# A hybrid attention layer with product-key experts: later gathers for one block, selection inside the dense experts, and weight buffers in another place

## The chip, the cores and the metric

One NeuronCore of a Trainium2 chip runs the whole layer. The time is device microseconds of one execution; what counts is the median of several. The engines are TensorE (PE; its weight loads are listed as PEld), VectorE (DVE), ScalarE (ACT), GpSimd (POOL) and SyncE (SP, which issues most transfers).

## What is computed

The layer has 1024 tokens of width 1024. Two attentions (differential attention with 8 heads of two maps, and chunked attention with 8 heads) are gated, projected and added to x, which gives h. Then each token is sent through 128 single-neuron experts out of 16384, and a last RMSNorm follows:

```python
def peer(xn, wq, keys, u, v):          # per block of 128 tokens
    q = (xb @ wq).reshape(PEER_BLOCK, PEER_HEADS, 2, PEER_DKEY // 2)
    v1, i1 = lax.top_k(s1, PEER_TOPK)  # scores against two key tables, 16 best of 128 each
    v2, i2 = lax.top_k(s2, PEER_TOPK)
    sc, ci = lax.top_k(cand, PEER_TOPK)            # 16 best sums of pairs
    e = i1[...] * PEER_NKEYS + i2[...]             # 8 heads x 16 experts
    g = jax.nn.softmax(sc, axis=-1)
    hid = jnp.einsum('thkd,td->thk', u[e], xb)     # first layer
    a = gelu(hid) * g
    return jnp.einsum('thk,thkd->td', a, v[e])     # second layer
h = h + peer(rmsnorm(h, norm2_w), ...)
y = rmsnorm(h, final_norm_w)
```

u and v are 16384 x 1024 float32 tables (64 MB each).

## The kernel before, in words

The tokens are eight blocks of 128. The experts are computed in two ways. **Blocks 0, 1, 6 and 7** (SBLK) are sparse: `experts(b)`, L789, gathers for each of the 128 expert slots the 128 rows of u that the tokens of the block chose (one indirect transfer of 512 KB, issued by GpSimd, L803), multiplies it with the tokens and sums along the row into `hid` (DVE, L809), and does the same with v (gather L803, accumulation into `acc` L815). Between the layers stand the gelu (L811) and the product with the gates (L812), behind them `final` (L781), the last norm and the store (L787). So a block has 256 gathers. The gathered rows go through five buffers (GBUFS, tag "ge" of the pool "gath"); `xs2`, `acc`, `hid`, `a` and `junk` have one buffer each. **Blocks 2 to 5** (DBLK) are dense: `dense_experts`, L681, goes through all 16384 experts in 128 chunks of 128. For a chunk SP loads a tile of u (transposed, L194 in `wtile`) and of v (L735); ScalarE and DVE split each into a high and a low part (`split`, L126: a copy to fp32r on ScalarE, L128, and the rest on DVE, L129); PE multiplies u's parts with the tokens' parts (24 matmuls, L136), ScalarE takes the gelu (L748), DVE multiplies with the gate matrix of the chunk (L749), both are split again, and the second layer (L710 and L717, 24 matmuls a chunk on average) adds up in PSUM. v is split in two halves of 512 columns, u in one piece.

The gate matrices are made ahead of this: `choose` (L565) selects the experts of a block on DVE in nine steps (it is a generator that yields after each), and `gates` (L643) turns the selection of a dense block into a matrix with 32 steps of four tokens, each with a copy L671 on ScalarE, and stores it to memory. For a sparse block `choose` ends with the index list `ei` (L639).

The order of the program is written by hand: generators are advanced by `weave` (L52), one step of the main one and so many of the others. After the attentions come `mop(2)` with the gates of blocks 2 and 3, `mop(3)` with the selection of 4 and 5 and their gates (L894, L895; `mop` and the `merge` that it calls make h, its norm and the query scores of two blocks), then the selection of blocks 6 and 7 (L897), the dense experts, and last the sparse blocks one after the other (L899). Below this a scheduler puts each engine's instructions in an order of its own: what stands later in the program may go ahead where an engine would be idle. So the gathers of block 0, last in the program, start some 340 us into the span, and blocks 6 and 7 run beside the dense experts. Each engine then works its list off in order. A tile takes one of the buffers of its tag, and waits for one to come free.

Pools are laid out one after the other: "wp" holds the raw, high and low parts of weights; "yza" and "tkp" hold what the selection needs; "dk" (L686) holds the dense stage's tiles and opens when the pools of the front (`fstack`, L896) are closed.

Of the kernel before, what the change touches and what calls it, by code (L numbers as in the profile page):

```python
# [7 lines left out]
F32 = mybir.dt.float32  # L8
F32R = mybir.dt.float32r
BF16 = mybir.dt.bfloat16  # L10
# [5 lines left out]
P = 128  # L16
# [56 lines left out]
def layer_kernel(ctx, tc, x, w1, w_in, b_gate, lq1, lk1, lq2, lk2, subln, rel,  # L73
# [3 lines left out]
    con = ctx.enter_context(tc.tile_pool(name="con", bufs=1))  # L77
    gp = ctx.enter_context(tc.tile_pool(name="gath", bufs=GBUFS))
    sms = ctx.enter_context(tc.tile_pool(name="sms", bufs=2))
    wp = ctx.enter_context(tc.tile_pool(name="wp", bufs=2))  # L80
    yza = ctx.enter_context(tc.tile_pool(name="yza", bufs=1))
    tkp = ctx.enter_context(tc.tile_pool(name="tkp", bufs=1))
    drp = ctx.enter_context(tc.tile_pool(name="dr", bufs=1, space=bass.MemoryType.DRAM))

    def load(pool, shape, src, name):
# [40 lines left out]
    def split(raw, hi, lo):  # L126

        nc.scalar.copy(hi, raw)  # L128
        nc.vector.tensor_sub(lo, raw, hi.bitcast(F32))  # L129
# [548 lines left out]
        for f in pend:  # L678
            f()

    def dense_experts():  # L681


        T = DT
        with ExitStack() as st:
            dk = st.enter_context(tc.tile_pool(name="dk", bufs=2))  # L686
            smd = st.enter_context(tc.tile_pool(name="smd", bufs=2))
            xh = dk.tile([P, KC, T], F32R, name="x2h", bufs=1)
            xl = dk.tile([P, KC, T], F32R, name="x2l", bufs=1)
            with tc.tile_pool(name="dps0", bufs=2, space=PSUM) as pt:  # L690
                for i, b in enumerate(DBLK):
                    xs = wp.tile([P, KC, P], F32, name="xd", tag="wr", bufs=WBUFS).rearrange("p a b -> p (a b)")
                    nc.sync.dma_start(xs, xn2d[b])
                    for g in range(2):
                        o = pt.tile([P, 512], F32, name="trd", tag="trd")
                        for j in range(4):
                            nc.tensor.transpose(o[:, j * P:(j + 1) * P], xs[:, (4 * g + j) * P:(4 * g + j + 1) * P], ident)
                        dst = (slice(None), slice(4 * g, 4 * g + 4), slice(i * P, (i + 1) * P))
                        split(cols4(o, 4), xh[dst], xl[dst])
            pd = st.enter_context(tc.tile_pool(name="dps", bufs=1, space=PSUM))  # L700
            acc = [[pd.tile([P, 512], F32, name=f"acc{i}{hf}") for hf in range(2)] for i in range(3)]
            rest = dk.tile([P, D], F32, name="rest", bufs=1)
            nc.sync.dma_start(rest, hd[DBLK[3]])

            def second(j, a, b):
                for x, y in ((0, 0), (0, 1), (1, 0)):
                    kw = dict(start=(j == 0 and x == y), stop=(j == NCH - 1 and x == 1))
                    for i in range(3):
                        for hf in range(2):
                            nc.tensor.matmul(acc[i][hf], a[x][:, i * P:(i + 1) * P], b[y][:, hf * 512:hf * 512 + 512], **kw)  # L710

            def fourth(hf, chunks):
                o = pd.tile([P, 512], F32, name="acc3", tag="acc3")
                cs = slice(hf * 512, hf * 512 + 512)
                todo = [(a[x], b[y]) for _, a, b in chunks for x, y in ((0, 0), (0, 1), (1, 0))]
                for n, (aa, bb) in enumerate(todo):
                    nc.tensor.matmul(o, aa[:, 3 * P:4 * P], bb[:, cs], start=(n == 0), stop=(n == len(todo) - 1))  # L717
                nc.vector.tensor_add(rest[:, cs], rest[:, cs], o)

            def sums(chunks):  # L720

                two = len(chunks) == 2
                if two:
                    fourth(0, chunks)
                second(*chunks[-1])
                if two:
                    fourth(1, chunks)
                    chunks.clear()

            chunks = []  # L730
            new = None
            for j in range(NCH):
                uw = wtile(ut[j])
                vr = dk.tile([P, D], F32, name="vr", tag="vr", bufs=RBUFS)
                nc.sync.dma_start(vr, v[j * P:(j + 1) * P, :])  # L735
                vh = dk.tile([P, D], F32R, name="vh", tag="vh", bufs=VBUFS)
                vl = dk.tile([P, D], F32R, name="vl", tag="vl", bufs=VBUFS)
                for hf in range(2):
                    cs = slice(hf * 512, hf * 512 + 512)
                    split(vr[:, cs], vh[:, cs], vl[:, cs])  # L740
                if j % JG == 0:
                    gj = dk.tile([P, T // TB, JG, TB], F32, name="gj", tag="gj")
                    for i in range(T // TB):
                        nc.sync.dma_start(gj[:, i], gdr[i][:, j:j + JG, :])
                ph = pd.tile([P, 512], F32, name="ph", tag="ph")
                mm3(ph, uw, (xh, xl), KC)
                ge = dk.tile([P, T], F32, name="ge", tag="ge")
                nc.scalar.activation(ge, ph, AF.Gelu)  # L748
                nc.vector.tensor_mul(ge.rearrange("p (n t) -> p n t", t=TB), ge.rearrange("p (n t) -> p n t", t=TB),  # L749
                                     gj[:, :, j % JG, :])  # L750
                ah = dk.tile([P, T], F32R, name="ah", tag="ah", bufs=ABUFS)
                al = dk.tile([P, T], F32R, name="al", tag="al", bufs=ABUFS)
                split(ge, ah, al)
                if new:
                    chunks.append(new)
                    sums(chunks)
                new = (j, (ah, al), (vh, vl))
            def last(tag, src):
                t = wp.tile([P, KC, P], F32, name="last", tag=tag).rearrange("p a b -> p (a b)")
                nc.sync.dma_start(t, src)  # L760
                return t

            hxs = [last("wh", hd[b]) for b in DBLK[:2]]
            wfb = last("wl", wf.to_broadcast([P, D]))
            chunks.append(new)
            sums(chunks)
            for i, b in enumerate(DBLK):
                hx = rest
                if i < 3:
                    if i < 2:  # L770
                        hx = hxs[i]
                    else:
                        hx = dk.tile([P, D], F32, name="hx", tag="vr", bufs=RBUFS)
                        nc.sync.dma_start(hx, hd[b])
                    for hf in range(2):
                        dst = hx[:, hf * 512:(hf + 1) * 512]
                        nc.vector.tensor_add(dst, dst, acc[i][hf])
                sq = wp.tile([P, KC, P], F32, name="sq", tag="wr", bufs=WBUFS).rearrange("p a b -> p (a b)")
                final(hx, sq, smd, b * P, wfb)
# [9 lines left out]
    def experts(b):  # L789

        ei, g = idx_of[b]
        K = P
        xs = gp.tile([P, D], F32, name="xs2", tag="xs2", bufs=1)
        nc.sync.dma_start(xs, xn2d[b])
        acc = gp.tile([P, D], F32, name="acc", tag="acc", bufs=1)
        nc.sync.dma_start(acc, hd[b])
        g = g.rearrange("p a b -> p (a b)")
        hid = gp.tile([P, P], F32, name="hid", tag="hid", bufs=1)[:, :K]
        junk = gp.tile([P, D], BF16, name="junk", tag="junk", bufs=1)

        def gather(src, k):
            t = gp.tile([P, D], F32, name="ge", tag="ge")
            nc.gpsimd.indirect_dma_start(out=t, out_offset=None, in_=src,  # L803
                                         in_offset=bass.IndirectOffsetOnAxis(ap=ei[:, k:k + 1], axis=0))
            return t

        for k in range(K):
            t = gather(u, k)
            nc.vector.scalar_tensor_tensor(junk, t, 1.0, xs, op0=OP.mult, op1=OP.mult, accum_out=hid[:, k:k + 1])  # L809
        a = gp.tile([P, P], F32, name="a", tag="a", bufs=1)[:, :K]  # L810
        nc.scalar.activation(a, hid, AF.Gelu)  # L811
        nc.vector.tensor_mul(a, a, g)  # L812
        for k in range(K):
            t = gather(v, k)
            nc.vector.scalar_tensor_tensor(acc, t, a[:, k:k + 1], acc, op0=OP.mult, op1=OP.add)  # L815
        wfb = gp.tile([P, D], F32, name="wfb", tag="ge")
        nc.sync.dma_start(wfb, wf.to_broadcast([P, D]))
        final(acc, junk, sms, b * P, wfb)

    dn = [None, None]  # L820
# [73 lines left out]
            weave(mop(2, mp, yzb), 26, (gates(gk, d1), 32 * len(d1)))  # L894
            weave(mop(3, mp, yza), 26, (chain(sel([4, 5], yzb), gates(gk, d2)), 18 + 32 * len(d2)))  # L895
    fstack.close()  # L896
    run(sel([6, 7], yza))  # L897
    dense_experts()
    for b in SBLK:  # L899
        experts(b)  # L900


# [49 lines left out]
```

## Time and profile before

| | us |
|---|---|
| median of 3 runs | 3390.54 |
| lowest and highest | 3386.21, 3400.17 |
| the profiled execution, its own time | 3385.27 |
| its span, first to last instruction | 3383.5 |
| mean granted clock of TensorE (share of full speed) | 0.955 |

The page of the profile gives the busy time of each engine and the chain of work that ended last, followed back from the last instruction. Busy time can also be read by stretch of the span, together with the granted clock of PE, the share of the 16 DMA engines and the GB/s that they moved. A timeline lists one engine's instructions by start, with the idle time before each and what released it. Names are the program's: out<-in.

### The profile page before, as it was taken

What the parts mean: (1) busy time and instruction counts of PE and PEld (TensorE: products, weight loads), DVE (VectorE), ACT (ScalarE), POOL (GpSimd) and SP (SyncE); (2) the same over time, 40 slices, a digit from 0 to 9 for tenths busy, and PEclk for the clock granted to TensorE, in tenths of its full rate; (3) what the DMA queues carried; (4) which work ended last, traced back from release to release, by engine and by line L of the source; (5) the groups of instructions that cost most, each with busy time, mean ns of one, the idle gap of its engine ahead of it and who ended that gap; (6) DMA issues with size and microseconds to landing.
All of it is one profiled execution on the core that took longest, in us unless ns stands there. A gap on an engine that the chain in (4) does not pass through costs nothing.

```text
span 3383.5 us, 48294 instructions
## 1 busy us (share of the span) xinstructions
PE 3101.4 (92%) x16032; PEld 2548.4 (75%) x16032; DVE 2696.5 (80%) x5848; ACT 1445.1 (43%) x3029; POOL 1249.5 (37%) x1028
## 2 busy tenths in 40 slices
PE   7997689999979886987787699999999999999998
PEld 7986578888857664676676578888888888888886
DVE  4436797777769999888885999888888888898843
ACT  5634433434324544567749833333323323322323
POOL 0000455555544532344100035555555555555400
PEclk9998899999989897998898899999999999999999
DMA  7675999999999975898744579999999999999841
GB/s 240 217 243 192 369 323 352 334 355 333 332 340 356 323 269 176 281 325 332 269 152 151 210 265 356 344 336 335 340 335 353 329 335 338 337 343 341 314 128 69
DMA packets 406122, 987.13 MB, mean 292 GB/s; under 512 B 43184, under 2 KB 188400, under 8 KB 403696
## 3 DMA queue, kind: packets, MB, share of 16 engines
q0 software_dynamic: 147456, 536.94, 44.8%
q1 hardware_dynamic: 258416, 447.11, 38.0%
q8 instruction: 126, 2.06, 0.2%
q14 instruction: 124, 1.02, 0.1%
HBM read 905.72 MB, written 78.15 MB: 291 GB/s over the span
## 4 chain that ended last, share of the span: by engine, by line
PE 75%; DVE 12%; DMA 5%; ACT 4%; issue 3%; POOL 1%; SPq 0%; DVEq 0%; POOLq 0%; ACTq 0%
PE ph L136 21%; PE mm L136 17%; PE acc L710 15%; PE mm L490 7%; PE acc L717 5%; PE sc L347 3%; PE pv L372 3%; PE tr L203 2%; DVE junk L809 1%; DMA ge<-in_u_dram,ei 1%; PE gg L669 1%; DVE acc L815 1%; DVE qs L561 1%; DVE iu L563 1%; DVE iu L560 1%
## 5 line engine op out<-in xcount | busy, mean ns | idle before, releaser
L803 POOL DMA_INDIRECT ge<-in_u_dram,ei x512 | 616.7, 1205 | 1258.1 <-DVE junk L809 380.3
L803 POOL DMA_INDIRECT ge<-in_v_dram,ei x512 | 632.6, 1236 | 686.9 <-DVE acc L815 469.3
L815 DVE SCALAR_TENSOR_TENSOR acc<-ge,a,acc 128x1024 f32<-128x1024 f32 x512 | 655.1, 1279 | 21.6 <-DMA ge<-in_v_dram,ei 15.9
L809 DVE SCALAR_TENSOR_TENSOR junk<-ge,xs 128x1024 bf16<-128x1024 f32 x512 | 624.1, 1219 | 50.9 <-DMA ge<-in_u_dram,ei 44.6
L129 DVE TENSOR_TENSOR wl<-wr,wh 128x1024 fp32r<-128x1024 f32 x232 | 283.4, 1222 | 215.8 <-ACT wh L128 110.7
L128 ACT CAST wh<-wr 128x1024 fp32r<-128x1024 f32 x232 | 243.4, 1049 | 404.8 <-PE ph L136 276.5
L136 PE MATMUL ph<-x2h,wh 128*128 128x512 f32 x1024 | 406.2, 397 | 8.8 <-DVE x2l L129 6.6
L136 PE MATMUL ph<-x2l,wh 128*128 128x512 f32 x1024 | 407.7, 398 | 0.0
L136 PE MATMUL mm<-xh,wh 128*128 128x256 f32 (+1 forms) x1248 | 372.1, 325 | 0.7 <-ACT st L286 0.6
L136 PE MATMUL mm<-xl,wh 128*128 128x256 f32 (+1 forms) x1248 | 367.0, 321 | 1.3 <-DVE xl L232 1.2
L136 PE MATMUL ph<-x2h,wl 128*128 128x512 f32 x1024 | 259.4, 395 | 0.0
L136 PEld LDWEIGHTS mm<-xh,wh 128*128 128x128 f32 x1248 | 237.0, 190 | 24.8 <-ACT st L286 3.1
L128 ACT CAST vh<-vr 128x512 fp32r<-128x512 f32 x256 | 140.0, 618 | 269.3 <-PE acc L717 244.5
L136 PEld LDWEIGHTS mm<-xl,wh 128*128 128x128 f32 x1248 | 236.6, 190 | 21.4 <-DVE xl L232 2.0
L136 PEld LDWEIGHTS ph<-x2h,wh 128*128 128x128 f32 x1024 | 193.4, 189 | 55.5 <-DVE x2l L129 7.0
L136 PE MATMUL mm<-xh,wl 128*128 128x256 f32 (+1 forms) x1248 | 234.5, 324 | 0.0
L136 PEld LDWEIGHTS ph<-x2l,wh 128*128 128x128 f32 x1024 | 193.6, 189 | 47.7
L136 PEld LDWEIGHTS ph<-x2h,wl 128*128 128x128 f32 x1024 | 192.0, 188 | 46.9
L347 PE MATMUL sc<-kt,qt 64*128 64x256 f32 (+3 forms) x608 | 200.7, 529 | 14.5 <-DVE mn L353 9.0
L128 ACT CAST ah<-ge 128x512 fp32r<-128x512 f32 x128 | 79.7, 622 | 294.9 <-DVE ge L749 294.9
L710 PE MATMUL acc<-vh,ah 128*128 128x512 f32 x768 | 198.8, 389 | 0.0
L136 PEld LDWEIGHTS mm<-xh,wl 128*128 128x128 f32 x1248 | 184.8, 190 | 16.8
(203 smaller groups left out, 5733.1 us busy)
## 6 DMA issues: line engine op xcount, KB each, us to landing
vr<-in_v_dram SPq DMA_DIRECT2D x128, 512.0 KB, 6.5
wr<-in_ut_dram SPq DMA_DIRECT2D x128, 512.0 KB, 5.8
wr<-in_w_in_dram SPq DMA_DIRECT2D x104, 512.0 KB, 5.3
gdr<-gst SPq DMA_DIRECT2D x16, 2048.0 KB, 8.7
gj<-gdr SPq DMA_DIRECT2D x512, 64.0 KB, 6.0
wr<-in_w_bd_dram SPq DMA_DIRECT2D x40, 512.0 KB, 4.2
wr<-in_w_out_dram SPq DMA_DIRECT2D x40, 512.0 KB, 7.4
wr<-in_wq_dram SPq DMA_DIRECT2D x40, 512.0 KB, 5.1
```

What stands on the lines that cost most here:

```text
L128: nc.scalar.copy(hi, raw)
L129: nc.vector.tensor_sub(lo, raw, hi.bitcast(F32))
L136: nc.tensor.matmul(o, w[a][:, k, :], xx[b][:, k, :], start=(i == 0), stop=(i == last))
L203: nc.tensor.transpose(o[:, i * P:(i + 1) * P], s, ident)
L347: nc.tensor.matmul(o[:, :k1 - k0], q, k[:, k0:k1], start=True, stop=True)
L372: nc.tensor.matmul(o[:, :P], aT[:, j - c, :], vt[:, v0 + j, :], start=(j == 0), stop=(j == n - 1))
L490: nc.tensor.matmul(o, w[:, k, :], xx[:, k, :], start=(k == 0), stop=(k == K - 1))
L710: nc.tensor.matmul(acc[i][hf], a[x][:, i * P:(i + 1) * P], b[y][:, hf * 512:hf * 512 + 512], **kw)
L717: nc.tensor.matmul(o, aa[:, 3 * P:4 * P], bb[:, cs], start=(n == 0), stop=(n == len(todo) - 1))
L803: nc.gpsimd.indirect_dma_start(out=t, out_offset=None, in_=src, in_offset=bass.IndirectOffsetOnAxis(ap=ei[:, k:k + 1], axis=0))
L809: nc.vector.scalar_tensor_tensor(junk, t, 1.0, xs, op0=OP.mult, op1=OP.mult, accum_out=hid[:, k:k + 1])
L815: nc.vector.scalar_tensor_tensor(acc, t, a[:, k:k + 1], acc, op0=OP.mult, op1=OP.add)
```

## The change

The pool "wp" is opened after "yza" and "tkp". In the dense experts v is split in one piece. The selection of blocks 6 and 7 is no longer run ahead of the dense experts but handed to them, three steps after each chunk's instructions. `experts` becomes a generator with a stop after the first layer and another in the middle of the second; it loads `acc` after the first stop and takes `junk` once more for the last norm. Block 0 runs as before; of block 1 the first layer and 64 gathers of the second follow, then block 6's first layer, the other 64 of block 1, and the rest of blocks 6 and 7.

```diff
@@ -77,9 +77,9 @@
     con = ctx.enter_context(tc.tile_pool(name="con", bufs=1))
     gp = ctx.enter_context(tc.tile_pool(name="gath", bufs=GBUFS))
     sms = ctx.enter_context(tc.tile_pool(name="sms", bufs=2))
-    wp = ctx.enter_context(tc.tile_pool(name="wp", bufs=2))
     yza = ctx.enter_context(tc.tile_pool(name="yza", bufs=1))
     tkp = ctx.enter_context(tc.tile_pool(name="tkp", bufs=1))
+    wp = ctx.enter_context(tc.tile_pool(name="wp", bufs=2))
     drp = ctx.enter_context(tc.tile_pool(name="dr", bufs=1, space=bass.MemoryType.DRAM))
 
     def load(pool, shape, src, name):
@@ -678,7 +678,7 @@
         for f in pend:
             f()
 
-    def dense_experts():
+    def dense_experts(side, per):
 
 
         T = DT
@@ -735,9 +735,7 @@
                 nc.sync.dma_start(vr, v[j * P:(j + 1) * P, :])
                 vh = dk.tile([P, D], F32R, name="vh", tag="vh", bufs=VBUFS)
                 vl = dk.tile([P, D], F32R, name="vl", tag="vl", bufs=VBUFS)
-                for hf in range(2):
-                    cs = slice(hf * 512, hf * 512 + 512)
-                    split(vr[:, cs], vh[:, cs], vl[:, cs])
+                split(vr, vh, vl)
                 if j % JG == 0:
                     gj = dk.tile([P, T // TB, JG, TB], F32, name="gj", tag="gj")
                     for i in range(T // TB):
@@ -755,6 +753,8 @@
                     chunks.append(new)
                     sums(chunks)
                 new = (j, (ah, al), (vh, vl))
+                for _ in range(per):
+                    next(side, None)
             def last(tag, src):
                 t = wp.tile([P, KC, P], F32, name="last", tag=tag).rearrange("p a b -> p (a b)")
                 nc.sync.dma_start(t, src)
@@ -792,8 +792,6 @@
         K = P
         xs = gp.tile([P, D], F32, name="xs2", tag="xs2", bufs=1)
         nc.sync.dma_start(xs, xn2d[b])
-        acc = gp.tile([P, D], F32, name="acc", tag="acc", bufs=1)
-        nc.sync.dma_start(acc, hd[b])
         g = g.rearrange("p a b -> p (a b)")
         hid = gp.tile([P, P], F32, name="hid", tag="hid", bufs=1)[:, :K]
         junk = gp.tile([P, D], BF16, name="junk", tag="junk", bufs=1)
@@ -807,14 +805,20 @@
         for k in range(K):
             t = gather(u, k)
             nc.vector.scalar_tensor_tensor(junk, t, 1.0, xs, op0=OP.mult, op1=OP.mult, accum_out=hid[:, k:k + 1])
+        yield
+        acc = gp.tile([P, D], F32, name="acc", tag="acc", bufs=1)
+        nc.sync.dma_start(acc, hd[b])
         a = gp.tile([P, P], F32, name="a", tag="a", bufs=1)[:, :K]
         nc.scalar.activation(a, hid, AF.Gelu)
         nc.vector.tensor_mul(a, a, g)
         for k in range(K):
+            if k == K // 2:
+                yield
             t = gather(v, k)
             nc.vector.scalar_tensor_tensor(acc, t, a[:, k:k + 1], acc, op0=OP.mult, op1=OP.add)
         wfb = gp.tile([P, D], F32, name="wfb", tag="ge")
         nc.sync.dma_start(wfb, wf.to_broadcast([P, D]))
+        junk = gp.tile([P, D], BF16, name="junk", tag="junk", bufs=1)
         final(acc, junk, sms, b * P, wfb)
 
     dn = [None, None]
@@ -894,10 +898,15 @@
             weave(mop(2, mp, yzb), 26, (gates(gk, d1), 32 * len(d1)))
             weave(mop(3, mp, yza), 26, (chain(sel([4, 5], yzb), gates(gk, d2)), 18 + 32 * len(d2)))
     fstack.close()
-    run(sel([6, 7], yza))
-    dense_experts()
-    for b in SBLK:
-        experts(b)
+    dense_experts(sel([6, 7], yza), 3)
+
+    e0, e1, e6, e7 = (experts(b) for b in SBLK)
+    run(e0)
+    next(e1)
+    next(e1)
+    next(e6)
+    for e in (e1, e6, e7):
+        run(e)
 
 
 # ---- launch: one core; inputs and outputs as the reference has them ----
```

## Rows read from the trace of the kernel before

**Rows 1.** The page: busy time by engine, and the chain by engine
```profile
PE 3101.4 (92%) x16032; PEld 2548.4 (75%) x16032; DVE 2696.5 (80%) x5848; ACT 1445.1 (43%) x3029; POOL 1249.5 (37%) x1028
...
PE 75%; DVE 12%; DMA 5%; ACT 4%; issue 3%; POOL 1%; SPq 0%; DVEq 0%; POOLq 0%; ACTq 0%
```

**Rows 2.** Busy time by stretch: length, PE, PEld, DVE, ACT, POOL, clock, DMA, GB/s
```profile
1489.00:1680.00 191.00, 158.84 (x946) 140.40 (x944) 167.80 (x422) 156.03 (x356) 63.25 (x50) 0.92 0.86 317
1750.00:1917.00 167.00, 138.16 (x831) 120.97 (x830) 115.57 (x450) 154.70 (x360) 0.00 (x0) 0.91 0.43 158
1680.00:1720.00 40.00, 20.15 (x78) 16.38 (x79) 39.78 (x229) 6.38 (x17) 0.00 (x0) 0.74 0.43 151
1917.00:1965.00 48.00, 22.50 (x78) 16.51 (x79) 45.02 (x199) 21.02 (x36) 0.00 (x0) 0.64 0.72 241
2200.00:3200.00 1000.00, 1000.00 (x4347) 815.60 (x4347) 886.07 (x1122) 306.46 (x462) 525.53 (x413) 1.00 0.96 339
3210.00:3310.00 100.00, 100.00 (x436) 81.53 (x435) 39.99 (x54) 33.02 (x52) 0.00 (x0) 1.00 0.38 116
```

**Rows 3.** The chain in order of time: start, us, what
```profile
1521.74 12.05 DMA ge<-in_v_dram,ei
...
1600.05 16.14 DMA rb<-rst
...
2014.78 5.59 PE ph L136 x24
...
3340.20 5.59 PE ph L136 x24
```

**Rows 4.** GpSimd's gathers and SP's stores in order of time [idle before <- releaser]
```profile
1664.35 1.14 POOL L803 DMA_INDIRECT ge<-in_v_dram,ei  x1 [6.40 <-DVE acc L815]
1971.59 0.93 POOL L803 DMA_INDIRECT ge<-in_u_dram,ei  x1 [306.10 <-DVE ei L639]
...
3193.87 0.94 POOL L803 DMA_INDIRECT ge<-in_v_dram,ei  x1 [2.19 <-DVE acc L815]
...
3212.95 0.34 SPq L787 DMA_DIRECT2D out_dram<-acc  x1
...
3379.41 0.33 SPq L787 DMA_DIRECT2D out_dram<-rest  x1
```

**Rows 5.** Gate copies and accumulations by stretch: ns min/median/max, first to last start
```profile
L671 ACT COPY gst<-gg x64: 1012/1056/1087, 1489.0 to 1678.1; 128x512 f32<-128x512 f32 x64
...
L671 ACT COPY gst<-gg x64: 994/1053/1092, 1750.6 to 1916.8; 128x512 f32<-128x512 f32 x64
...
L815 DVE SCALAR_TENSOR_TENSOR acc<-ge,a,acc x54: 1261/1276/1285, 1489.6 to 1683.7; 128x1024 f32<-128x1024 f32 x54
```

**Rows 6.** PE in order of time, scores of attention and query
```profile
1170.25 0.79 PE L347 MATMUL sc<-kt,qt 64*128 64x128 f32 x2
...
1179.56 1.94 PE L203 MATMUL tr<-ident,xs 128*128 128x128 f32 x8 [6.94 <-DVE f L391]
...
1193.43 0.72 PE L547 MATMUL sc<-keyT,st 64*128 64x128 f32 x8
1193.98 1.02 PE L347 MATMUL sc<-kt,qt 64*128 64x512 f32 x2
```

**Rows 7.** The handover: first load, first matmul, the splits of x2
```profile
1925.22 0.32 SPq L703 DMA_DIRECT2D rest<-hd  x1
...
1948.07 0.80 PE L136 MATMUL ph<-x2h,wh 128*128 128x512 f32 x1 [6.60 <-DVE x2l L129]
...
L128 ACT CAST x2h<-trd x8: 575/578/592, 1925.3 to 1942.2; 128x512 fp32r<-128x512 f32 x8
L129 DVE TENSOR_TENSOR x2l<-trd,x2h x8: 668/690/705, 1926.4 to 1947.3; 128x512 fp32r<-128x512 f32 x8
```

**Rows 8.** Splits late in the dense stage, DVE
```profile
3332.11 2.49 DVE L129 TENSOR_TENSOR vl<-vr,vh 128x512 fp32r<-128x512 f32 x4
...
3335.53 1.23 DVE L129 TENSOR_TENSOR wl<-wr,wh 128x1024 fp32r<-128x1024 f32 x1 [0.93 <-ACT wh L128]
```

## The prediction

> **What bounds the kernel now.** I read the page first. TensorE (PE) is busy 92% of the span and carries 75% of the chain that ended last; VectorE (DVE) carries 12% of it [rows 1]. A mean over the span hides the stages, so the busy time by stretch comes next [rows 2]. From 2200 to 3200 us PE is busy 1000 of 1000 us at clock 1.00: the dense experts are bound by PE. In the chain their pieces recur every 22.09 us, two chunks: (3340.20 - 2014.78) / 60 [rows 3], so 128 chunks cost 128 x 11.045 = 1414 us however DVE and the transfers fare, as long as these keep up. Ahead of them PE has holes. In the first batch of gate matrices (1489 to 1680) DVE is the fullest engine (167.8 of 191 us), in the second (1750 to 1917) ScalarE (154.7 of 167), from 1680 to 1720 DVE alone (39.8 of 40), and from 1917 to 1965, the handover to the dense experts, PE has 22.5 of 48 us at clock 0.64 [rows 2].
>
> GpSimd's gathers are the other stream. Block 1's last one is issued at 1664.35, then nothing for 306 us until block 6's indices exist, and the last gather of all at 3193.87; its block's result is stored at 3212.95 [rows 4]. The dense experts run to 3383.5, so the gathers end some 170 us early, yet in the first gates batch they hold up DVE: transfers of gathered rows (12.05 us) and a broadcast beside them (16.14 us) stand in the chain there [rows 3]. The change trades that slack for that hold-up.
>
> **Does the order hold?** Block 1's late gathers now stand behind block 6's first layer in the program, but nothing in their data makes them wait. What could is the tag of their five buffers. Another tag shows how buffers are given out: attention scores and the query scores of L547 share "sc". The last score of an attention step runs at 1170.25, and its successors use the same loaded head, yet PE idles 6.94 us before 1179.56 and no score runs until L547 has had its turn at 1193.43; attention follows at 1193.98 [rows 6]. So buffers of a tag go out in the order of the program, even where the earlier user isn't ready, and I take it that the 64 gathers wait.
>
> **The change, term by term**, against the profiled execution (span 3383.5, time 3385.27, so 1.8 us around it; the median of the runs shown is 5.3 us above).
>
> *Front, 64 gathers gone.* The two gates batches run the same code over 64 steps: 1489.0 to 1678.1 is 189.1 us with 50 gathers beside it, 1750.6 to 1916.8 is 166.2 us with none [rows 2, 5]. Difference 22.9 us. Behind the first batch, in the stretch that DVE fills, two accumulations and block 1's final multiply leave too: 3 x 1.28 = 3.8 us. Gain 27 us. Ends: nothing, if ScalarE (156.0 of 191 us) is already the limit; not below, as nothing new is put there; and 54 x 1.276 + 1.28 = 70 us, if all of the DVE time comes off [rows 5]. I take the twin batch, the nearest row.
>
> *Handover.* The last gate copy starts at 1916.8 [rows 5]; the dense pool opens at 1925.22, when the first load into it is issued; the first dense matmul waits until 1948.07 for a split (x2l) [rows 7]. DVE is busy 45.0 of 48 us there [rows 2], much of it with blocks 6 and 7's selection, which now stands behind chunks 0 to 5 (18 steps, three a chunk). Alone, eight splits of 0.58 (ScalarE) + 0.69 us (DVE) take 10.2 us, so 1935.5 [rows 7]; two or three more for the first weights gives 1938. Gain 10 us; ends 12.6 and, if a selection step held up the second chunk in turn, a loss of one chunk, 11 us. I take 10, as the waits named are DVE's.
>
> *Selection later.* Block 6's indices come later against the start of the dense work, since the splits go first: some nine DVE instructions of 0.69 us, 6 us. Ends 0 and 22 us (two chunks).
>
> *Splits of v joined.* Four half splits back to back take 2.49 us on DVE and one whole 1.23, so 128 x (1.245 - 1.23) = 2 us [rows 8]. ScalarE does as many fewer and is busy 306 of 1000 us there, all of it beside a full PE [rows 2]: nothing. Without that cover the 2 us would be a gain, and waiting for the whole of v a loss of half a split, 0.6 us a chunk. The Trainium skill, "VectorE: DVE Perf Modes" (Side-by-side: where the cycles go), gives each instruction about 150 cycles of start, by which 128 fewer would be an estimated 20 us of DVE. The row, 0.62 us for half and 1.23 for whole, does not agree for instructions that follow each other; the sum goes by the row.
>
> *Weight buffers moved.* Only addresses change. The same split takes 1.245 us per 1024 columns on the dense buffers and 1.23 on the weight buffers [rows 8], so place costs nothing visible: 0, with 128 x 0.015 = 2 us either way.
>
> *SP's queue.* Block 1's broadcast load and its store move into the dense stage, and blocks 1, 6 and 7 load their accumulator after the first layer: some five issues of 0.33 us among the dense loads. The one accumulator buffer makes block 6's load wait for block 1's store, and dense loads queue behind it. Before, block 7's load did the same behind block 6's store with PE at 1000 of 1000 [rows 2], so nothing; without that cover, about 4 us, the time from the last store to the end of the span (3379.41 to 3383.5) [rows 4].
>
> *Sums.* Dense work ends at 3383.5 - 27 - 10 = 3346.5. The gathers: now 512 in 3193.87 - 1971.59 = 1222.3 us, 2.392 us each [rows 4]; after, 576, the first at 1971.6 - 27 + 6 = 1950.6; the last 575 x 2.392 = 1375.4 later; then 19.1 us to the store and 4.1 to land [rows 4]: 3349. The two ends almost meet; the later one counts. Time 3349 + 1.8 = 3351 against the profiled 3385.27, or 3356 on the scale of the median, which I predict.
>
> **The rivals.** *The gathers set the end, and late.* They sit at the limit of the transfers already: 339 GB/s at a share of 0.96, against 116 GB/s of the dense work alone [rows 2]. If block 6's indices come two chunks late (22 us), the front gains nothing and the pace is that of 2200 to 3200 (413 gathers in 1000 us, 2.42), the first gather is at 1994 and the end at 1994 + 575 x 2.42 + 23.2 = 3409: 3416 on the median's scale, slower than before. It decides once the first gather comes later than about 1984 at 2.392. For: no slack is left; against: DVE starts the selection in the 8 us in which the dense pool is still shut [rows 7]. The Trainium skill, "DMA: Bandwidth & Descriptors" (Specifications), puts the memory's limit per core at about 358 GB/s; the trace, at 339, is 5% under it. By that limit an estimate is 2.2 us for a gather, and the gathers would end well ahead of the dense work.
>
> *The gathers aren't held back.* If the scheduler gives the buffers to whoever is ready, block 1 ends near 1690 as now and only the handover gains: 3383.5 - 10 = 3373.5, or 3381 on the median's scale. For: the scheduler does put block 0's gathers, last in the program, far ahead; against: [rows 6].
>
> *The front gains all of its DVE time*, 70 us: dense work ends at 3303, the gathers at 1907.6 + 1398.6 = 3306, time 3313. For: DVE is full from 1680 to 1720 [rows 2]; against: the twin batch, bound by ScalarE.
>
> **How the numbers follow.** Half a percent, 17 us, is about what a measurement of this kernel can tell from no change: faster means under 3373.6, slower over 3407.5. Forecast 0.53, its own range 3338 to 3373: faster. Front gains all, 0.10: faster. Not held back, 0.15: within half a percent. Late gathers, 0.22: 0.12 slower, 0.10 where the delay only eats the gain. So 0.63, 0.25, 0.12. The range runs from 3325 to 3405; outside are the upper part of the late gathers and the far part of the full gain.
>
> **What would show it.** Right: no gather between about 1465 and 1945; the first gates batch near 166 us; first dense matmul 10 us closer to the last gate copy; 576 gathers in the dense stage, at 2.39 us; the last store within 10 us of the end; PE still 1000 of 1000 in between. Wrong: gathers of block 1 on until 1660 (not held back); a first gather of block 6 more than 70 us behind the last gate copy, or a wait for GpSimd's results at the end of the chain (late gathers); or new gaps of PE in the dense stage, in which I count none.

## The result, and the profile after

| | before | changed |
|---|---|---|
| median of four runs, us | 3390.55 | 3343.39 |
| lowest and highest | 3386.21, 3400.17 | 3342.99, 3344.66 |
| ratio, 95% interval | | 0.9853 [0.9838, 0.9867] |
| profiled execution: time, span | 3385.27, 3383.5 | 3344.66, 3342.9 |

47 us or 1.5% faster; the prediction said 34.5 us faster. (In the changed kernel L801 is the gather, L807 the first layer's sum and L818 the accumulation; before they were L803, L809 and L815.) The page after, its engines and its chain (before: [rows 1]):

```profile
PE 3083.5 (92%) x16032; PEld 2551.2 (76%) x16032; DVE 2689.5 (80%) x5720; ACT 1430.6 (43%) x2901; POOL 1289.7 (39%) x1028
...
PE 71%; DVE 11%; DMA 5%; ACT 5%; issue 5%; POOL 2%; SPq 0%; DVEq 0%; POOLq 0%; ACTq 0%
```

TensorE does the same 16032 matmuls in 18 us less busy time. That is the first line which no term of the prediction explains. Busy time by stretch, cut at the two gates batches, the stretch between them, the handover and the dense work (columns as in [rows 2]):

```profile
1495.00:1673.00 178.00, 155.76 (x948) 137.95 (x946) 117.02 (x441) 156.42 (x362) 0.00 (x0) 0.93 0.51 181
1673.00:1728.00 55.00, 41.41 (x181) 35.43 (x182) 53.07 (x247) 15.23 (x34) 0.00 (x0) 0.88 0.53 172
1728.00:1898.00 170.00, 143.82 (x860) 126.08 (x858) 116.18 (x454) 155.54 (x361) 0.00 (x0) 0.92 0.43 159
1898.00:1946.00 48.00, 21.82 (x76) 16.25 (x77) 44.61 (x190) 20.32 (x32) 0.00 (x0) 0.61 0.71 241
2200.00:3200.00 1000.00, 1000.00 (x4414) 828.30 (x4413) 891.58 (x1033) 308.52 (x388) 560.23 (x418) 1.00 0.96 344
```

POOL shows x0 in all four stretches of the front: the gathers are held back. In the dense stage TensorE is still busy 1000 of 1000 us at clock 1.00, but it starts 4414 matmuls there and not 4347 [rows 2]. The chain in order of time (start, us, what) shows the period of one chunk in two, which was 22.09 us [rows 3]:

```profile
1951.85 5.44 PE ph L136 x24
...
1973.61 5.44 PE ph L136 x24
```

21.76 us. The 24 matmuls of u's parts take 5.44 us where they took 5.59; 18 matmuls of the second layer, `acc L710 x18`, take 4.08 us in both traces. Gate copies by stretch, as in [rows 5]:

```profile
L671 ACT COPY gst<-gg x64: 1018/1050/1125, 1495.3 to 1672.1; 128x512 f32<-128x512 f32 x64
...
L671 ACT COPY gst<-gg x64: 990/1052/1095, 1728.2 to 1897.6; 128x512 f32<-128x512 f32 x64
```

The first dense matmul, GpSimd's first and last gather of the dense stage, and SP's stores of the last sparse and the last dense block (before: [rows 4, 7]):

```profile
1929.83 0.79 PE L136 MATMUL ph<-x2h,wh 128*128 128x512 f32 x1 [6.97 <-DVE x2l L129]
```
```profile
1952.24 0.94 POOL L801 DMA_INDIRECT ge<-in_u_dram,ei  x1 [488.91 <-DVE ei L639]
...
3311.68 0.94 POOL L801 DMA_INDIRECT ge<-in_v_dram,ei  x1 [0.66 <-DVE acc L818]
```
```profile
3326.26 0.34 SPq L787 DMA_DIRECT2D out_dram<-acc  x1
...
3338.81 0.33 SPq L787 DMA_DIRECT2D out_dram<-rest  x1
```

The 488.91 us of idle time in front of the first gather of block 6 replace 306.10 us: block 1's late gathers did wait, though nothing in their data made them. The chain that ended last now runs through the last gathers, which the prediction had listed as a sign of late gathers:

```profile
3311.68 7.39 DMA ge<-in_v_dram,ei
```

Yet they cost nothing here: behind 1940 us PE has no idle time over 1 us, and from the start of its last matmul to the end of the span it is 14.4 us, against 15.5 before. Between the two profiled executions the last gate copy moved 19.2 us ahead (1916.8 to 1897.6), the way from there to the first dense matmul grew from 31.3 to 32.2 us, and from that matmul to the end of the span it went from 3383.5 - 1948.07 = 1435.4 to 3342.9 - 1929.83 = 1413.1 us. 19.2 - 0.9 + 22.3 = 40.6, the difference of the spans; the medians differ by 47.

### The profile page after: what moved, and what is told of

It is laid out like the page before. It is cut to its first block, busy times and chain, and to the rows that moved or that the text cites. A ratio compares the mean times of both kernels' runs of the same rounds, so it can differ in the third digit from the quotient of the medians.

```text
span 3342.9 us, 48089 instructions
## 1 busy us (share of the span) xinstructions
PE 3083.5 (92%) x16032; PEld 2551.2 (76%) x16032; DVE 2689.5 (80%) x5720; ACT 1430.6 (43%) x2901; POOL 1289.7 (39%) x1028
## 4 chain that ended last, share of the span: by engine, by line
PE 71%; DVE 11%; DMA 5%; ACT 5%; issue 5%; POOL 2%; SPq 0%; DVEq 0%; POOLq 0%; ACTq 0%
PE ph L136 18%; PE mm L136 17%; PE acc L710 13%; PE mm L490 8%; PE acc L717 4%; PE sc L347 4%; PE pv L372 3%; PE tr L203 2%; POOL ge L801 2%; PE gg L669 2%; DVE junk L807 1%; ACT gst L671 1%; DMA ge<-in_u_dram,ei 1%; DVE p L353 1%; DVE iu L560 1%
## 5 line engine op out<-in xcount | busy, mean ns | idle before, releaser
L801 POOL DMA_INDIRECT ge<-in_u_dram,ei x512 | 634.0, 1238 | 1419.0 <-DVE ei L639 830.4
L801 POOL DMA_INDIRECT ge<-in_v_dram,ei x512 | 655.5, 1280 | 603.6 <-DVE acc L818 397.3
L818 DVE SCALAR_TENSOR_TENSOR acc<-ge,a,acc 128x1024 f32<-128x1024 f32 x512 | 655.6, 1280 | 24.3 <-DMA ge<-in_v_dram,ei 17.5
L807 DVE SCALAR_TENSOR_TENSOR junk<-ge,xs 128x1024 bf16<-128x1024 f32 x512 | 624.4, 1219 | 47.3 <-DMA ge<-in_u_dram,ei 41.3
L136 PE MATMUL ph<-x2l,wh 128*128 128x512 f32 x1024 | 399.8, 390 | 0.0
L128 ACT CAST vh<-vr 128x1024 fp32r<-128x1024 f32 x128 | 128.5, 1052 | 249.5 <-PE acc L717 226.5
L710 PE MATMUL acc<-vh,ah 128*128 128x512 f32 x768 | 197.6, 389 | 0.0
```

What stands on the lines that cost most here:

```text
L136: nc.tensor.matmul(o, w[a][:, k, :], xx[b][:, k, :], start=(i == 0), stop=(i == last))
```

## The experiments

All times are beside runs of the kernel before on the same chip, and each ratio is to these. A run built on the changed kernel is compared with it by its ratio; each ratio is known to 0.1 to 0.2%, 3 to 6 us.

### One part at a time: weight pool, split of v, order, selection

**e1**, the weight pool alone:

```diff
-    wp = ctx.enter_context(tc.tile_pool(name="wp", bufs=2))
     yza = ctx.enter_context(tc.tile_pool(name="yza", bufs=1))
     tkp = ctx.enter_context(tc.tile_pool(name="tkp", bufs=1))
+    wp = ctx.enter_context(tc.tile_pool(name="wp", bufs=2))
```

> The kernel before with one edit: the weight pool opens behind the pools of the selection, as in the change. Every engine gets the same instructions in the same order as before; only addresses differ. In the changed kernel two dense chunks take about 21.77 us instead of 22.09, because the 24 matmuls of u's parts start every 227 ns instead of 233. Theory A (the address of the weight tiles): the chunks go at 21.77, dense matmuls take 64 x 0.32 = 20 us less, the gathers still end early, time about 3370. Theory S (the joined split of v frees something that the matmuls share): chunks stay at 22.09, time 3390, within 0.2%.

Measured: 3378.83 us, ratio 0.9954 [0.9938, 0.9971]. **e2**, `split(vr, vh, vl)` in place of the two halves, alone:

> The kernel before with one edit: v split in one piece of 1024 columns. Theory A (addresses): two chunks stay at 22.09 us, matmuls of u's parts start every 233 ns, DVE's splits of v take 1.22 us each instead of twice 0.62 to 0.69, time 3390 within 0.2%. Theory S (the joined split): chunks at 21.77, matmuls every 227 ns, time about 3370.

Measured: 3393.89 us, ratio 1.0002 [0.9992, 1.0012]. The stretch of 1000 us in e1, then in e2:

```profile
2200.00:3200.00 1000.00, 1000.00 (x4414) 828.30 (x4413) 899.15 (x1142) 312.81 (x471) 529.83 (x418) 1.00 0.96 343
```
```profile
2200.00:3200.00 1000.00, 1000.00 (x4347) 814.84 (x4346) 879.31 (x1034) 298.57 (x372) 564.14 (x415) 1.00 0.95 338
```

e1 has the 4414 matmuls of the changed kernel, e2 the 4347 of before. So the addresses bring the faster chunks, with every engine's instructions unchanged. The joined split frees DVE (886.07 [rows 2] to 879.31 us in 1000) and gives no time.

**e5**, the order of the sparse blocks alone (the change's `experts` and the lines that advance e0, e1, e6, e7; the rest as before):

```diff
-    for b in SBLK:
-        experts(b)
+    e0, e1, e6, e7 = (experts(b) for b in SBLK)
+    run(e0)
+    next(e1)
+    next(e1)
+    next(e6)
+    for e in (e1, e6, e7):
+        run(e)
```

> The kernel before with the sparse blocks as in the change (block 1's last 64 gathers behind block 6's first layer, acc loaded after the first layer) and nothing else: selection of 6 and 7 ahead of the dense work, v split in halves, weight pool in its old place. The prediction gave this part 27 us, nearly all in the first gates batch. In the changed kernel the last gate copy starts 19 us earlier than before, 12 of it in that batch and 16 between the batches, less 9 elsewhere. Theory F (the order alone makes the front shorter): last gate copy 15 to 27 us closer to the start of the first batch, chunks still at 22.09, time 15 to 27 us under the kernel before. Theory W (the woven selection is needed too, as it takes DVE work out of the front): under 10 us.

Measured: 3362.82 us against 3393.07, ratio 0.99 [0.9883, 0.9917], 30 us. The gate copies run from 1495.9 to 1897.8; the first dense matmul:

```profile
1931.36 0.80 PE L136 MATMUL ph<-x2h,wh 128*128 128x512 f32 x1 [7.35 <-DVE x2l L129]
```

The front ends where that of the changed kernel does (its last gate copy starts at 1897.6). Theory F holds; the 30 us lie a little over its 15 to 27. **e6**, the selection alone:

```diff
-    def dense_experts():
+    def dense_experts(side, per):
...
                 new = (j, (ah, al), (vh, vl))
+                for _ in range(per):
+                    next(side, None)
...
-    run(sel([6, 7], yza))
-    dense_experts()
+    dense_experts(sel([6, 7], yza), 3)
```

> The kernel before with the selection of blocks 6 and 7 handed to the dense experts, three steps behind each chunk, and nothing else. The prediction gave this part 10 us, as the splits of x2 would no longer wait for DVE. Theory P (as predicted): first dense matmul 21 us behind the last gate copy instead of 31, time 10 us less. Theory N (nothing): the scheduler puts selection steps into DVE's idle time ahead of the splits either way; in the changed kernel the distance is 32 us; time within 3 us of the kernel before.

Measured: 3395.23 us, ratio 1.0001 [0.9987, 1.0014]; the last gate copy starts at 1939.1 and the first dense matmul at 1970.84, 31.7 us apart:

```profile
1970.84 0.79 PE L136 MATMUL ph<-x2h,wh 128*128 128x512 f32 x1 [6.75 <-DVE x2l L129]
```

Theory N holds. Of the four parts two do all of it: the order 1.0% and the addresses 0.5%, together the 1.5% measured.

### What of the address matters

The next six kernels get unused bytes ahead of the weight pool, behind it, or both. The edit is a pool of its own, here of 32 bytes a partition ahead:

```diff
+    pad0 = ctx.enter_context(tc.tile_pool(name="pad0", bufs=1))
+    nc.vector.memset(pad0.tile([P, 8], F32, name="pad0"), 0.0)
     wp = ctx.enter_context(tc.tile_pool(name="wp", bufs=2))
```

**e3** and **e4**, 32 bytes ahead and 32 behind, in the changed kernel and in the one before:

> The changed kernel with 32 bytes a partition put ahead of the weight pool and 32 behind it. The weight tiles stay next to the dense ones, but start at an odd multiple of 32 bytes (wh at 102560 instead of 102528), as they did in the kernel before (81504); the dense tiles move by 64 and keep their remainder. Theory A1 (what matters is that the stationary tile starts at a multiple of 64 bytes): matmuls of u's parts at 233 ns, two chunks at 22.09, time 3343 + 20 = 3363. Theory A2 (what matters is the place, next to the dense tiles): 227 ns, 21.77, time 3343.

> The kernel before with 32 bytes a partition put ahead of the weight pool and 32 behind it: the weight tiles keep their old place far from the dense ones, but start at multiples of 64 bytes (wh at 81536 instead of 81504). Theory A1 (a start at a multiple of 64 bytes): matmuls of u's parts at 227 ns, two chunks at 21.77, time 3390 - 20 = 3370. Theory A2 (the place): 233 ns, 22.09, time 3390.

Measured: e3 3358.36 us, ratio 0.9886 [0.9869, 0.9902], 4348 matmuls in the 1000 us; e4 3379.08, 0.9945 [0.9929, 0.9962], 4386 matmuls, half way. (By time alone e4 can't be told from e1; by its trace the stretch from the first dense matmul to the end is 1425.1 us, between 1435.4 before and 1414.3 in e1.) A start at a multiple of 64 bytes seemed to explain e3 and most of e4. **e7**, 32 bytes ahead alone, in the changed kernel:

> The changed kernel with 32 bytes a partition put ahead of the weight pool and nothing behind it: weight tiles and dense tiles all start at a remainder of 32 (of 128 bytes). So far the dense matmuls started every 227 ns with stationary and moving tiles both at remainder 0, every 233 with 96 and 0 or 32 and 64, and every 229 with 0 and 64. Theory R (what counts is that both start at the same remainder): 227 ns in both layers, as in the changed kernel, time like it. Theory Q (what counts is that each starts at a multiple of 64 or 128): now the second layer's matmuls are slow too, 48 a chunk at some 233 ns, 128 x 48 x 6.3 ns = 39 us more than the changed kernel.

Measured: 3343.95 us, 0.985 [0.9831, 0.9869], 4413 matmuls. None of the weight and dense tiles starts at a multiple of 64 any more and nothing is lost, so theory A1 falls. **e8**, 32 ahead and 96 behind, in the kernel before:

> The kernel before with 32 bytes ahead of the weight pool and 96 behind it: the weight tiles keep their far place, and weight and dense tiles all start at multiples of 128 bytes. With 32 and 32 bytes (dense tiles at remainder 64) the matmuls of u's parts started every 229 ns, between the 233 of before and the 227 of the changed kernel. Theory A1 (the remainders alone): 227 ns, two chunks at 21.77 us, dense matmuls 20 us shorter than before, as with the weight pool moved. Theory A3 (the place has a part of it): 229 ns again.

Measured: 3399.96 us, 1.0018 [1.0005, 1.0031], 4343 matmuls. Weight and dense tiles all start at multiples of 128 and the matmuls are slow: A1 falls once more, and so does theory R, by which equal remainders of 128 are enough. What was left is the distance between the two operands, as a remainder of more than 128, or the far place. **e9**, 480 bytes behind the weight pool in the kernel before, and **e10**, 256 behind it in the changed one:

> The kernel before with 480 bytes put behind the weight pool and nothing else: the weight tiles stay far from the dense tiles and at their old addresses, but the distance from wh to x2h becomes 29696 bytes, 58 times 512. So far the dense matmuls started every 227 ns where the distance of the starts was a multiple of 512 (8192 in the changed kernel and with all tiles at remainder 32; 53248 in the second layer), and slower where it left a remainder of 512: 32 (233 ns, twice), 64 (229), 128 (233). Theory D (the remainder of the distance): 227 ns, two chunks at 21.77 us, time 20 us under the kernel before. Theory P (near or far): 233 ns, as before.

> The changed kernel with 256 bytes put behind the weight pool: the distance from wh to x2h becomes 8448, a remainder of 256 of 512 bytes. Theory D512 (only multiples of 512 are free of the cost): matmuls of u's parts at 229 to 233 ns, time 8 to 20 us over the changed kernel. Theory D256 (multiples of 256 do): 227 ns, time like the changed kernel.

Measured: e9 3373.93 us, 0.9941 [0.9924, 0.9957], 4414 matmuls; e10 3343.54 us, 0.985 [0.9833, 0.9868], 4413 matmuls. The stretch in e8 and in e9, which differ in nothing but unused bytes:

```profile
2200.00:3200.00 1000.00, 1000.00 (x4343) 816.54 (x4342) 883.98 (x1129) 309.49 (x467) 531.78 (x414) 1.00 0.95 338
```
```profile
2200.00:3200.00 1000.00, 1000.00 (x4414) 828.02 (x4413) 899.01 (x1140) 312.82 (x471) 532.11 (x417) 1.00 0.96 343
```

All of them, by the distance in bytes from the start of wh to that of x2h, as the built programs have it; ns is the mean from one start to the next behind matmuls of u's parts, from the starts in the traces between 2200 and 3200 us:

| kernels | distance | remainder of 256 | ns |
|---|---|---|---|
| before, e2, e5, e6 | 29216 | 32 | 232 to 234 |
| e3 | 8224 | 32 | 232 to 234 |
| e4 | 29248 | 64 | 229 |
| e8 | 29312 | 128 | 233 |
| changed, e1, e7, e11, e12 | 8192 | 0 | 227 |
| e10 | 8448 | 0 | 227 |
| e9 | 29696 | 0 | 227 |

The matmul reads wh as stationary and x2h as moving operand. Where their starts lie a multiple of 256 bytes apart a matmul starts every 227 ns, near or far; at the other remainders tried (32, 64, 128) it takes 2 to 7 ns more. The pads move every dense tile against every weight tile, so the table alone doesn't single out these two operands; e11 below, with other tiles, makes them the likely pair. What in the chip does this no run here shows; that the next weight load and the running matmul meet in the memory is only a guess. The Trainium skill, "TensorE: Matmul & The Clock Gate" (Step-by-step: what each phase is for), says "Loading the next tile's weights doesn't steal SBUF read bandwidth from the running matmul." If the guess is right, these runs don't quite agree with it: 3% of a matmul of 512 columns.

**e11** carries this to the front of the changed kernel, where the same weight tiles meet xh and xl:

```diff
+        xp.tile([P, 24 if T > 256 else 48], F32, name="xpad", tag="xpad")
         xh = xp.tile([P, KC, T], F32R, name="xh", tag="xh")
```

> The changed kernel with 96 and 192 bytes put ahead of the tiles xh of the front, so that the distance from wh and wl to xh and xl is a multiple of 512 there too (it left 416 and 224). The front's matmuls of x with the split weights take 231 to 232 ns at 512 columns and 116 at 256; some 1100 and 2250 of them follow another of their kind. Theory D (the remainder): 227 and 114 ns, 10 us less TensorE time ahead of 1450 us, of which the stretches in which TensorE is the fullest engine give back 3 to 10 us: 3333 to 3340 against 3343. Theory N (only the dense tiles show it): the same durations and time as the changed kernel.

Measured: 3344.49 us, 0.9859 [0.9843, 0.9876], like the changed kernel. By the starts in the trace (median), the matmuls of 512 columns, some 1200, went from 234 to 227 ns, but those of 256 columns, some 2400, from 117 or 118 to 120. Added up over the starts, the former take 283.4 us in place of 289.9 and the latter 296.8 in place of 293.2: 6.5 us gained and 3.6 lost, too little for the time to tell. Theory D holds for 512 columns alone; there the front also adds remainders 160 (changed), 192 (before) and 224 (e4), with 233 to 234 ns each. With 256 columns remainder 0 is as slow as any seen, also in the kernel before, whose first group of tokens has it (120) and whose second has remainder 192 (114).

### The handover

**e12**, the changed kernel with block 7's selection made to wait for the last split of x2 (it adds zero times a number of x2l to a score):

```diff
+            for b in (7,):
+                e = top1[b][0][:, 0, 0, 0:1]
+                nc.vector.scalar_tensor_tensor(e, xl[:, KC - 1, T - 1:T].bitcast(F32), 0.0, e, op0=OP.mult, op1=OP.add)
             pd = st.enter_context(tc.tile_pool(name="dps", bufs=1, space=PSUM))
```

> The changed kernel with block 7's selection held back: one number of its scores is rewritten as itself plus zero times the last x2l, so that none of its selection can run on VectorE before the splits of x2 are done; block 6's selection stays as it is. In the changed kernel the first dense matmul comes 32 us behind the last gate copy, although the selection stands behind chunks 0 to 5 in the program, and selection steps of both blocks stand between the eight splits of x2l. Theory V (VectorE's selection steps hold the splits up, as the prediction's handover term had it, and the change failed to move them): some 25 instructions of 0.27 us leave the stretch, the first matmul comes 25 to 27 us behind the last gate copy, block 6's first gather no later than now, time 3 to 6 us under the changed kernel. Theory L (the loads and transposes of x2 set the pace, or block 6's steps alone do): 31 to 32 us, the same time.

Measured: 3351.12 us beside 3398.36 for the kernel before, ratio 0.9852 [0.9835, 0.9869], as for the change itself. First dense matmul, then block 6's first gather, then the last sparse and the last dense store of its trace; its last gate copy starts at 1905.1:

```profile
1930.74 0.80 PE L136 MATMUL ph<-x2h,wh 128*128 128x512 f32 x1 [3.06 <-DVE x2l L129]
```
```profile
1964.71 0.94 POOL L804 DMA_INDIRECT ge<-in_u_dram,ei  x1 [492.80 <-DVE ei L639]
```
```profile
3345.52 0.33 SPq L790 DMA_DIRECT2D out_dram<-acc  x1
...
3347.91 0.33 SPq L790 DMA_DIRECT2D out_dram<-rest  x1
```

The first dense matmul comes 25.6 us behind the last gate copy instead of 32.2, so theory V is right about the splits. But block 6's first gather now comes 59.6 us behind that copy, against 54.6 in the changed kernel. The last sparse block is stored 2.4 us ahead of the last dense one, where it was 12.6 ahead: the gathers have moved into the end. From the first dense matmul to the end of the span the trace has 1421.3 us instead of 1413.1, which eats up the 6.6. Some 2 of the 8 us lie in the first 16 chunks; 1.5 are a wait of PE, at 3331.98, for an addition of DVE that stands behind the gathers' accumulations; and from the start of the last matmul to the end it is 18.8 us instead of 14.4, where block 7's last norm now stands among the dense ones. The medians, known to some 6 us, could not tell 3 to 6 us from nothing. What was expected of the first gather is a miss, and the forecast gain of 3 to 6 us isn't seen.

## Why the prediction came out as it did

Direction and range were right, and the sum was off by 12.6 us of 47. On the scale of the profiled executions, dense work was forecast to end at 3346.5 and ended at 3342.9. That these are only 3.6 us apart is luck: the front gave 7.8 us less than forecast there and the handover 10.9 less, and 22.3 us came from the dense stage, which had been given nothing. Of the rest 2.5 us are the gathers, which were forecast as the later end (3349) and came first: the last sparse store is issued at 3326.26. The last 6.6 are the two executions that were profiled, the one before 5.3 us under its median and the changed one 1.3 over. Of the signs of being right, the empty stretch without gathers, the 576 gathers behind it and the full PE came; the first batch near 166 us (176.8), the first dense matmul 10 us closer (0.9 farther) and the last sparse store within 10 us of the end (16.6) did not.

**Buffers in the program's order: right.** The 488.91 us of idle time ahead of block 6's first gather show it, and with it the reading of [rows 6]. The rival "not held back" is out.

**Front, forecast 27 us: right in sum, wrong in its places.** Seven traces have block 1's gathers in the front (before, e1, e2, e4, e6, e8, e9), seven have them behind (the changed kernel, e3, e5, e7, e10 to e12). From the first gate copy to the last they agree within 3 us among themselves:

| | with the gathers | without | gain |
|---|---|---|---|
| first batch, us | 188.9 to 189.8 | 175.8 to 176.8 | 13 |
| between the batches | 70.8 to 72.7 | 56.0 to 56.1 | 16 |
| second batch | 165.5 to 166.2 | 169.3 to 169.7 | -3.5 |

That is some 25.5 us. The failing step is "I take the twin batch, the nearest row", which gave 22.9 us to the first batch. That batch isn't the twin: in its new form it still has PE 155.8 and ScalarE 156.4 of 178 us, where the second has PE 138.2 of 167 [rows 2]. DVE's relief there (167.8 of 191 to 117.0 of 178 us) let selection run early instead (its searches, L559 to L563, number 147 there and 103 before, the short loads that go with them not counted), and the stretch between, which DVE fills (53.1 of 55 us), lost 16 us, not 3.8: 82 DVE instructions left it (247 now, 329 between 1679 and 1750 before), two accumulations and a final multiply among them, the others searches of the selection. The rest of e5's 30 us may lie ahead of the first gate copy, which starts anywhere from 1489.0 to 1510.6 in the first seven traces (mean 1500.4) and from 1490.0 to 1503.2 in the others (mean 1494.8); no run takes that part by itself. The profiled execution of before is the earliest of the first seven, so its front was a flattering base.

**Handover, forecast 10 us: nothing.** The failing step is "selection, which now stands behind chunks 0 to 5". The text of the program has it there; the scheduler lets later work go ahead on an idle engine, as the section on the kernel says. DVE is busy 44.6 of 48 us with the same work, and the wait is still 6.97 us on x2l. e6 shows that the weave alone does nothing. e12 shows that the price was fair (6.6 us for one block's steps) and that most of it is lost again where the gathers and the dense work end together.

**Weight buffers moved, forecast 0: 16 to 20 us by the times of e1 and e9, 20 to 22 by the dense stages of the traces.** This is the step that failed most: "Only addresses change". It was priced by a row of DVE [rows 8], while the engine that reads these tiles at the bound is PE; and that row compared two halves with one whole instruction (in the changed kernel a whole split takes 1.22 us on either pool), so it told nothing of the place. "128 chunks cost 1414 us however DVE and the transfers fare" went with it. The sign stood in the profile of before, in two rows of the page's groups of PE that the prediction didn't set side by side:

```profile
L136 PE MATMUL ph<-x2h,wh 128*128 128x512 f32 x1024 | 406.2, 397 | 8.8 <-DVE x2l L129 6.6
...
L710 PE MATMUL acc<-vh,ah 128*128 128x512 f32 x768 | 198.8, 389 | 0.0
```

Same columns, clock 1.00, all back to back, and yet 8 ns apart.

**Split of v, forecast 0: right** (e2), with more DVE freed than the row gave: (886.07 - 879.31) x 1.414 = 10 us, not 2. The busy time of these splits says the same: 164 us for 256 halves in e1, 153.5 for 128 wholes in e2. The estimate of 20 us by the Trainium skill's page "VectorE: DVE Perf Modes" (Side-by-side: where the cycles go) is as far off on the other side. **Selection 6 us later: not seen**, the first gather comes 22.4 us behind the first dense matmul, 23.5 before. **SP's queue, forecast 0:** no gap of PE in the dense stage.

**Gathers.** 575 steps take 3311.68 - 1952.24 = 1359.4 us, 2.364 each instead of 2.392, and by the sum this kept the late gathers from setting the end: at 2.392 the last would have come 16 us later, and its block's store with it, behind that of the last dense block (3338.81). The pace went with the chunks: it is 2.39 to 2.40 us in before, e2, e3, e5, e6 and e8, and 2.36 to 2.37 in the seven traces at 227 ns. Per chunk that is 11.045 / 2.392 = 4.62 gathers before and 10.88 / 2.364 = 4.60 after. So the gathers follow the dense work, and the sum of the prediction had treated the two as independent. That DVE's list ties them, where the instructions of both stand between one another, fits this but no run tests it. The rival of late gathers had its mechanism right: e12 begins to meet it with 5 us of delay, though the dense store is still the last.

## What to carry to other kernels

Where a stage is full on TensorE, compare the start-to-start time of its matmuls of equal shape; if one kind is slower, look at the distance between its stationary and moving tiles before the schedule, since a pad of a few hundred bytes may be worth it (here 0.5%), and measure it for each column count. A step that is moved later in the program has not moved if a scheduler fills idle engines; read where its instructions are listed, or tie it by data. And when one stream's slack has been spent on another, the next gain of a few us ahead of it can be lost to the first, as in e12.

## What the runs showed of the hardware

- Matmuls of fp32r with 512 columns start every 226.7 ns where the stationary and the moving tile are a multiple of 256 bytes apart, every 229 at a remainder of 64, every 232 to 234 at 32 and at 128, at clock 1.00 throughout (means between 2200 and 3200 us). In the front, by medians, 512 columns give 233 to 234 ns at remainders 160, 192 and 224 as well and 227 at 0; with 256 columns remainder 0 gives 120 ns, 160 gives 118, 224 gives 117 and 192 gives 114.
- Freeing an engine that isn't the only full one gave a quarter: the first batch got 13 us shorter for 50.8 us less of DVE (167.8 to 117.0), with ScalarE at 156 us in both.
- The gathers' pace follows the dense chunks (4.62 and 4.60 a chunk) although the transfers' share is 0.96 at either pace.
